# Low parts, loads and stores of two MLP products: which engine or queue makes them

## The chip, the core and the metric

The kernel runs on one core of a Trainium2 chip. A core has five engines, each with an instruction stream that runs in order: TensorE (PE in the profile; its weight loads are PEld), VectorE (DVE), ScalarE (ACT), GpSimd (POOL) and SyncE (SP). Transfers are issued from a stream too: plain loads from SP, and from POOL the stores and the accumulating loads, which add what they bring to what the tile holds. Sixteen DMA engines carry them. The metric is device time in microseconds.

## The reference

Two residual sub-layers over 1024 tokens of width 1024: a mixer (an RG-LRU and an S5 state space group), and then an MLP with a squared ReLU. Only the MLP is touched:

```python
x = layer_norm(DEEPNORM_ALPHA * x + g1 * m_lat, ln1_g[l], ln1_b[l])
f_lat = sq_relu_mlp(modulate(x, sh2, sc2), mlp_w1[l], mlp_b1[l], mlp_w2[l], mlp_b2[l])
x = layer_norm(DEEPNORM_ALPHA * x + g2 * f_lat, ln2_g[l], ln2_b[l])

def sq_relu_mlp(x, w1, b1, w2, b2):
    return jnp.square(jax.nn.relu(x @ w1 + b1)) @ w2 + b2
```

`w1` is 1024 x 4096, `w2` is 4096 x 1024, all in fp32.

## The kernel before

**Three products for one.** An fp32 operand is split into a high part `wh`, which ScalarE casts to the matmul type fp32r, and a low part `wl`, the remainder. A product is then high x high, high x low and low x high: three matmuls of 128x128 by 128x512.

**Seven products for eight.** Both MLP matrices are cut into 2 x 2 blocks and multiplied by a scheme of seven block products, named "1" to "7". Their operands are blocks or sums of blocks, and the results are added up in several steps.

**First product.** `w1` comes as 32 tiles of [128, 1024], two to a pair, 16 pairs. Product "2" of all pairs is made early, while the mixer ends, and its result goes to a DRAM scratch, `p2scr`. The other six follow in a loop over `stream`: for each pair p the products "1", "6", "7", "4", "5", "3", each of 12 matmuls into one PSUM bank (`part_product`, L1061 to L1067). `combo_next` (L1126) prepares operands four products ahead. `operand` builds the sums of w1 blocks on VectorE (`st`, `wr`). For "6", "7", "5" and "3" the low part is a VectorE subtraction. "1" and "4" are plain blocks of w1, and theirs comes another way:

```python
if n in "14":
    S.activation(lo, f(hi), AF.Copy, scale=-1.0)
    G.dma_start(out=lo, in_=a["w1"][2 * p + (n == "4")][:, HS[n == "4"]], accum_op=ADD)
```

that is, ScalarE writes minus the high part (L1137), and an accumulating load from POOL's queue adds the block of w1 to it, 256 KB (L1138). The tiles `wh` and `wl` hold two operands each and have three buffers, so six operands, one pair.

**What follows a product.** VectorE adds the PSUM bank to the running sums `u` and `r`; ScalarE applies ReLU and square into `hq`, four hidden blocks of a pair; after "3" VectorE adds four sums of hidden blocks (the operands of the second product) to the same tile, and POOL stores block 0 (L1187, 256 KB) and blocks 2 to 7 (L1188, 1.5 MB). Beside this, for 14 of the 16 pairs, two tiles of `w2` are loaded (`we` 512 KB, `wo` 256 KB, one buffer each), VectorE makes a sum of three of its blocks, and POOL stores that in `sscr` (L1195).

**Second product.** Seven products of seven units each (the 14 pairs). A unit loads a [128, 1024] tile of w2 into `wr` (three buffers), for "7", "5" and "3" a second one into `by`, which VectorE adds or subtracts; it splits the sum into `wh` and `wl`, loads the hidden block `br`, splits that into `bh` and `bl`, and runs 24 matmuls (L1267). `unit_next` prepares a unit ahead. `finish` (L1248) takes a finished quarter of the result through the residual: it loads a tile `nin`, scales and shifts it on VectorE (a tensor_scalar) and adds it to `acc`. The last two pairs, without the scheme, are added at the end (`weights2`, `hidden`, L1347).

**Order.** A scheduler places each engine's instructions by data and buffers, and the engines then run them in that order; an instruction that waits holds up all behind it on its engine or queue.

Of the kernel before, what the change touches and what calls it, by code (L numbers as in the profile page):

```python
# [7 lines left out]
F32 = mybir.dt.float32  # L8
# [33 lines left out]
def build(nc, tc, a, out):  # L42
# [15 lines left out]
    def ld(o, i):  # L58
        return nc.sync.dma_start(out=o, in_=i)
# [7 lines left out]
    def f(t):  # L67
        return t.bitcast(F32)
# [1003 lines left out]
    for p in range(0, NP1 + 4, 2):  # L1072
# [7 lines left out]
        for e in range(2):  # L1080
# [3 lines left out]
            t = ap_.tile([P, 512], F32, tag="r", name="p2", bufs=6)  # L1084
# [19 lines left out]
    raws, sums = {}, {}  # L1104

    def raw_of(i):
        if i not in raws:
            raws[i] = wp.tile([P, 1024], F32, tag="wr", name="wr", bufs=3)
            ld(raws[i], a["w1"][i])
        return raws[i]  # L1110

    def operand(n, p):
        if n == "1":
            x, y = raw_of(2 * p), raw_of(2 * p + 1)
# [11 lines left out]
    def combo_next():  # L1126
        while len(c_ahead) < 4 and c_n[0] < len(stream):
# [8 lines left out]
            if n in "14":  # L1136
                S.activation(lo, f(hi), AF.Copy, scale=-1.0)  # L1137
                G.dma_start(out=lo, in_=a["w1"][2 * p + (n == "4")][:, HS[n == "4"]], accum_op=ADD)  # L1138
            else:
                tt(lo, src_, f(hi), SUB)  # L1140
# [4 lines left out]
    us_, t1, hq = {}, {}, {}  # L1145

    def rt():
        return ap_.tile([P, 512], F32, tag="r", name="r", bufs=6)
# [5 lines left out]
    for n, p in stream:  # L1154
        w = combo_next()
        ps = bank(512, "ps_m1")
        part_product(ps, w, XS[n], True, True)
        if n == "1":

            hq[p] = a2.tile([P, 8, 512], F32, tag="hq", name="hq", bufs=2)  # L1160
            u = us_[p] = a1.tile([P, 2, 512], F32, tag="u", name="u", bufs=2)
            v, t = rt(), rt()
            ld(v, p2scr[p])
            S.copy(t, ps)
            tt(v, t, v, ADD)
            act(0, v, hq[p][:, 0])
        elif n == "6":
            tt(u[:, 1], ps, t, ADD)
        elif n == "7":
            tt(u[:, 0], ps, u[:, 1], ADD)  # L1170
        elif n == "4":
            v = rt()
            tt(v, ps, u[:, 0], ADD)
            act(1, v, hq[p][:, 3])
        elif n == "5":
            tt(u, ps.unsqueeze(1).to_broadcast([P, 2, 512]), u, ADD)
            act(1, u[:, 0], hq[p][:, 2])
        elif n == "3":
            tt(u[:, 1], ps, u[:, 1], ADD)
            act(0, u[:, 1], hq[p][:, 1])  # L1180
            h = hq[p]
            if p < NPAIR:
                tt(h[:, 4:6], h[:, 1:3], h[:, 0:2], SUB)
                tt(h[:, 6], h[:, 2], h[:, 4], SUB)
                tt(h[:, 7], h[:, 3], h[:, 6], SUB)
                hv = hscr[p // 2].rearrange("i p k c -> p i k c")[:, :, p % 2]
                G.dma_start(out=hv[:, 0], in_=h[:, 0])  # L1187
                G.dma_start(out=hv[:, 2:8], in_=h[:, 2:8])  # L1188
# [264 lines left out]
```

## Time and profile before

| | us |
|---|---|
| median of 3 runs (1666.52 to 1676.39) | 1667.84 |
| the profiled execution's own time | 1675.67 |
| its span, first to last instruction | 1673.9 |
| stretch of the first MLP product | 967 to 1324 |
| second MLP product | 1324 to 1615 |
| rest | 1615 to 1674 |

| engine | busy us | share of the span |
|---|---|---|
| PE | 1504.9 | 90% |
| DVE | 1258.8 | 75% |
| ACT | 850.6 | 51% |
| POOL | 74.7 | 4% |

A row of the profile's groups names a line of the kernel, an engine, an operation, output and inputs by the names of their tiles, and a count; behind it stand the busy time, the mean of one, and the idle time ahead of it with what ended that. PEclk is the granted clock of TensorE as a share of full speed. A busy TensorE may thus still run at less than its full clock. Line numbers of helpers (L47, a VectorE operation on two tensors; L59, a load on SP) hold many different operations, so names of tiles tell them apart.

### The profile page before, as it was taken

The page shows a single profiled execution, that of the slowest core. Times are in us where ns is not written, and L with a number is a line of the kernel's source. Part 1 is how long each engine was busy: PE and PEld are TensorE (multiplying, and loading weights), DVE is VectorE, ACT ScalarE, POOL GpSimd, SP SyncE. Part 2 cuts the span into 40 slices and gives each one's busy share as a digit, 9 for nine tenths or more (in the row PEclk, how much of TensorE's full clock was granted, in tenths as well). Part 3 has the DMA queues.
Part 4 walks back from the last instruction along what each step waited for, and adds up shares of the span by engine and source line. Part 5 has one row for each costly group of instructions (what it writes and reads, how often), then busy time and mean ns, then how long its engine had stood idle before and what let it go on. Part 6 is the DMA issues. An engine that isn't in the chain of part 4 may idle for free.

```text
span 1673.9 us, 20450 instructions
## 1 busy us (share of the span) xinstructions
PE 1504.9 (90%) x7148; PEld 1222.3 (73%) x7148; DVE 1258.8 (75%) x2546; ACT 850.6 (51%) x1194; POOL 74.7 (4%) x129
## 2 busy tenths in 40 slices
PE   7899998999879997899997997877888899999897
PEld 2687777777758786888786775666766688787687
DVE  7899999998949897449787885656565446658967
ACT  4666666666882327643335754435454433333315
POOL 0000000000000000000000121111111000000000
PEclk9999999999999999899999998888898999999898
DMA  7533333333745838837685777786665776867712
GB/s 255 209 117 110 104 107 116 116 122 120 266 161 160 224 114 201 200 141 237 210 269 163 240 211 228 246 252 194 176 176 168 248 249 211 282 206 249 267 44 101
DMA packets 138470, 312.55 MB, mean 187 GB/s; under 512 B 16384, under 2 KB 47616, under 8 KB 136960
## 3 DMA queue, kind: packets, MB, share of 16 engines
q1 hardware_dynamic: 109152, 245.31, 46.1%
q0 software_dynamic: 15168, 48.24, 9.9%
q10 hardware_dynamic: 14048, 17.70, 3.0%
q8 instruction: 56, 0.92, 0.2%
q14 instruction: 46, 0.38, 0.1%
HBM read 231.58 MB, written 79.63 MB: 186 GB/s over the span
## 4 chain that ended last, share of the span: by engine, by line
PE 34%; DVE 27%; DMA 17%; issue 11%; ACT 10%; POOL 1%; SPq 0%; ACTq 0%; DVEq 0%; POOLq 0%
PE ps_m L1267 13%; PE ps_mm L380 4%; PE ps_m L1066 4%; DMA wr<-in_w 4%; PE ps_g L435 3%; DMA mo<-in_ada_t 3%; DVE wl L47 3%; DVE sT L47 2%; DMA wl<-in_w 2%; DVE xc L56 2%; DVE ii L47 2%; PE ps_m L1347 2%; ACT H L603 2%; DVE sU L47 1%; DVE H L47 1%
## 5 line engine op out<-in xcount | busy, mean ns | idle before, releaser
L98 ACT CAST wh<-wr 128x1024 fp32r<-128x1024 f32 x113 | 118.6, 1052 | 256.5 <-PE ps_m L1267 84.5
L47 DVE TENSOR_TENSOR wl<-wr,wh 128x1024 fp32r<-128x1024 f32 (+1 forms) x129 | 148.7, 1154 | 90.9 <-ACT wh L98 80.4
L1066 PE MATMUL ps_m<-xt,wh 128*128 128x512 f32 x512 | 160.6, 396 | 0.0
L1267 PE MATMUL ps_m<-bh,wh 128*128 128x512 f32 x392 | 155.0, 397 | 5.4 <-ACT bh L1229 3.1
L1267 PE MATMUL ps_m<-bh,wl 128*128 128x512 f32 x392 | 153.0, 394 | 2.7 <-DVE wl L47 2.7
L1267 PE MATMUL ps_m<-bl,wh 128*128 128x512 f32 x392 | 154.1, 393 | 0.0
L380 PE MATMUL ps_mm<-x0h,wl 128*128 128x512 f32 x352 | 141.2, 402 | 0.9 <-DVE wl L47 0.9
L380 PE MATMUL ps_mm<-x0h,wh 128*128 128x512 f32 x352 | 141.0, 400 | 1.0 <-ACT wh L98 1.0
L380 PE MATMUL ps_mm<-x0l,wh 128*128 128x512 f32 x352 | 140.5, 399 | 0.0
L1066 PE MATMUL ps_m<-x,wl 128*128 128x512 f32 x128 | 62.4, 488 | 59.0 <-DMA wl<-in_w 59.0
L1066 PEld LDWEIGHTS ps_m<-xt,wh 128*128 128x128 f32 x512 | 99.2, 194 | 21.9 <-ACT wh L1135 0.2
L1066 PE MATMUL ps_m<-xt,wl 128*128 128x512 f32 x256 | 100.2, 393 | 1.0 <-DMA wl<-in_w 1.0
L1066 PE MATMUL ps_m<-x,wh 128*128 128x512 f32 x256 | 94.7, 456 | 0.0
L1267 PEld LDWEIGHTS ps_m<-bh,wh 128*128 128x128 f32 x392 | 74.8, 191 | 22.9 <-ACT bh L1229 3.6
L1267 PEld LDWEIGHTS ps_m<-bh,wl 128*128 128x128 f32 x392 | 74.3, 190 | 18.4 <-DVE wl L47 3.1
L1267 PEld LDWEIGHTS ps_m<-bl,wh 128*128 128x128 f32 x392 | 74.7, 191 | 15.9 <-issue 0.2
L675 PE MATMUL ps_wo<-ms,wh 128*128 128x512 f32 x256 | 81.1, 397 | 1.8 <-ACT ms L799 0.9
L1066 PEld LDWEIGHTS ps_m<-x,wl 128*128 128x128 f32 x128 | 29.7, 232 | 72.5 <-DMA wl<-in_w 65.6
L380 PEld LDWEIGHTS ps_mm<-x0h,wl 128*128 128x128 f32 x352 | 67.4, 192 | 14.3 <-DVE wl L47 1.4
L380 PEld LDWEIGHTS ps_mm<-x0h,wh 128*128 128x128 f32 x352 | 67.6, 192 | 13.7 <-ACT wh L98 1.4
L380 PEld LDWEIGHTS ps_mm<-x0l,wh 128*128 128x128 f32 x352 | 67.6, 192 | 12.9
L47 DVE TENSOR_TENSOR sT<-al,H 128x128 f32<-128x128 f32 x254 | 66.5, 284 | 1.3
(347 smaller groups left out, 3775.2 us busy)
## 6 DMA issues: line engine op xcount, KB each, us to landing
wr<-in_w SPq DMA_DIRECT2D x86, 512.0 KB, 4.4
br<-hq SPq DMA_DIRECT2D x49, 512.0 KB, 4.9
hq<-hq POOLq DMA_DIRECT2D x14, 1536.0 KB, 8.7
mo<-in_ada_t SPq DMA_DIRECT2D x32, 512.0 KB, 3.9
wr<-in_w_in SPq DMA_DIRECT2D x24, 512.0 KB, 4.5
wr<-in_w_out SPq DMA_DIRECT2D x24, 512.0 KB, 4.5
xt<-xt ACTq DMA_DIRECT2D x16, 512.0 KB, 2.7
yd<-Y SPq DMA_DIRECT2D x16, 512.0 KB, 2.6
```

The source lines that it names most:

```text
L47: (eng or V).tensor_tensor(out=o, in0=x, in1=y, op=op)
L56: V.scalar_tensor_tensor(out=o, in0=x, scalar=s, in1=y, op0=op0, op1=op1, **kw)
L98: S.copy(hi, raw)
L380: PE.matmul(ps, w[:, ks], x, start=(k == 0 and c == 0), stop=(k == KT - 1 and c == 2))
L435: PE.matmul(ps, w[:, w0:w0 + P], x[:, src:src + n], start=(c == 0), stop=(c == 2))
L603: S.copy(hv[0:64], ps[0:64])
L675: PE.matmul(ps, u[:, ks], v[:, js], start=(c == 0), stop=(c == 3 * KT - 1))
L1066: PE.matmul(ps, u[:, ks], v, start=(first and c == 0), stop=(last and c == 11))
L1267: PE.matmul(pss[m], w[:, 512 * k + P * m:512 * k + P * m + P], x[:, 512 * k:512 * k + 512], start=(q == 0 and k == 0 and c == 0), stop=(q ...
L1347: PE.matmul(ps, w[:, m * P:(m + 1) * P], x[:, js], start=(c == 0), stop=(c == 3 * len(hs) - 1))
```

## The change

In the first product:

- The low parts of "1" and "4" are made by VectorE like all others; the negation and the accumulating load are gone.
- `load_pair` loads a pair's two w1 tiles, its `p2` block and its two w2 tiles when "4" of the pair before is prepared. The w1 tiles have five buffers, three `wr` and two `wr2`; `p2t` has two; `we` and `wo` keep one.
- The first hidden block adds PSUM to `p2t` directly, where it took ScalarE's copy of it.
- The sum of w2 blocks is made after "7" into a tile of its own, `w2s` (one buffer), with its sign turned, and the products that use it follow.
- `hq` holds four blocks, and the four sums get a tile `hs` (one buffer). The stores are block 0 after "6" (256 KB), blocks 2 and 3 after "3" (512 KB), and `hs` (1 MB).

In the second product "5" and "3" get their sum from an accumulating load by POOL (14 of 512 KB) and no `by`; "7" keeps it. `finish` scales `nin` on ScalarE.

```diff
@@ -1081,7 +1081,7 @@
             es_ = slice(512 * e, 512 * e + 512)
             ps = bank(512, "ps_p2")
             part_product(ps, (wh[:, es_], wl[:, es_]), x0[1::2], True, True)
-            t = ap_.tile([P, 512], F32, tag="r", name="p2", bufs=6)
+            t = ap_.tile([P, 512], F32, tag="r", name="p2", bufs=4)
             S.copy(t, ps)
             G.dma_start(out=p2scr[p - 4 + e], in_=t)
     for _ in steps:
@@ -1101,17 +1101,31 @@
         return t.rearrange("p (k c) -> p k c", k=2)
 
     stream = [(n, p) for p in range(NP1) for n in "167453"]
-    raws, sums = {}, {}
-
-    def raw_of(i):
-        if i not in raws:
-            raws[i] = wp.tile([P, 1024], F32, tag="wr", name="wr", bufs=3)
+    raws, sums, p2t, w2t = {}, {}, {}, {}
+
+    def load_pair(p):
+        for i in (2 * p, 2 * p + 1):
+            pl_, tag, bf = (wp, "wr", 3) if i % 5 < 3 else (a1, "wr2", 2)
+            raws[i] = pl_.tile([P, 1024], F32, tag=tag, name="wr", bufs=bf)
             ld(raws[i], a["w1"][i])
-        return raws[i]
+
+        p2t[p] = a1.tile([P, 512], F32, tag="p2", name="p2t", bufs=2)
+        ld(p2t[p], p2scr[p])
+        if p < NPAIR:
+            e = a1.tile([P, 1024], F32, tag="we", name="we", bufs=1)
+            o = a1.tile([P, 512], F32, tag="wo", name="wo", bufs=1)
+            ld(two(e), a["w2"][2 * p:2 * p + 2, :, HI].rearrange("k p c -> p k c"))
+            ld(o, a["w2"][2 * p][:, LO])
+            w2t[p] = e, o
 
     def operand(n, p):
         if n == "1":
-            x, y = raw_of(2 * p), raw_of(2 * p + 1)
+            if p == 0:
+                load_pair(0)
+        if n == "4" and p + 1 < NP1:
+            load_pair(p + 1)
+        if n == "1":
+            x, y = raws[2 * p], raws[2 * p + 1]
             s2, s3, s4 = (a1.tile([P, 512], F32, tag="st", name=f"st{i}", bufs=4) for i in range(3))
             tt(s3, x[:, LO], y[:, LO], SUB)
             tt(y[:, LO], y[:, LO], y[:, HI], ADD)
@@ -1133,19 +1147,13 @@
             src_ = operand(n, p)
             hi, lo = (x[:, HS[c % 2]] for x in c_tile[0])
             S.copy(hi, src_)
-            if n in "14":
-                S.activation(lo, f(hi), AF.Copy, scale=-1.0)
-                G.dma_start(out=lo, in_=a["w1"][2 * p + (n == "4")][:, HS[n == "4"]], accum_op=ADD)
-            else:
-                tt(lo, src_, f(hi), SUB)
+            tt(lo, src_, f(hi), SUB)
             c_ahead.append((hi, lo))
         return c_ahead.pop(0)
 
     XS = {"1": x0[0::2], "5": xt_[0], "6": xt_[1], "7": xt_[2], "3": x1, "4": xt_[3]}
-    us_, t1, hq = {}, {}, {}
-
     def rt():
-        return ap_.tile([P, 512], F32, tag="r", name="r", bufs=6)
+        return ap_.tile([P, 512], F32, tag="r", name="r", bufs=4)
 
     def act(e, v, dst):
         S.activation(v, v, AF.Relu, bias=col("b1", 2 * p + e))
@@ -1155,46 +1163,46 @@
         w = combo_next()
         ps = bank(512, "ps_m1")
         part_product(ps, w, XS[n], True, True)
+        hv = hscr[p // 2].rearrange("i p k c -> p i k c")[:, :, p % 2] if p < NPAIR else None
         if n == "1":
 
-            hq[p] = a2.tile([P, 8, 512], F32, tag="hq", name="hq", bufs=2)
-            u = us_[p] = a1.tile([P, 2, 512], F32, tag="u", name="u", bufs=2)
-            v, t = rt(), rt()
-            ld(v, p2scr[p])
+            h = a2.tile([P, 4, 512], F32, tag="hq", name="hq", bufs=2)
+            u = a1.tile([P, 2, 512], F32, tag="u", name="u", bufs=2)
+            v, t = p2t.pop(p), rt()
             S.copy(t, ps)
-            tt(v, t, v, ADD)
-            act(0, v, hq[p][:, 0])
+            tt(v, ps, v, ADD)
+            act(0, v, h[:, 0])
         elif n == "6":
             tt(u[:, 1], ps, t, ADD)
+            if hv is not None:
+                G.dma_start(out=hv[:, 0], in_=h[:, 0])
         elif n == "7":
             tt(u[:, 0], ps, u[:, 1], ADD)
+            if hv is not None:
+                e, o = w2t.pop(p)
+                w2s = a1.tile([P, 512], F32, tag="ws", name="w2s", bufs=1)
+                tt(e[:, LO], e[:, LO], e[:, HI], ADD)
+                tt(w2s, o, e[:, LO], SUB)
+                G.dma_start(out=sscr[p // 2][:, p % 2], in_=w2s)
         elif n == "4":
             v = rt()
             tt(v, ps, u[:, 0], ADD)
-            act(1, v, hq[p][:, 3])
+            act(1, v, h[:, 3])
         elif n == "5":
             tt(u, ps.unsqueeze(1).to_broadcast([P, 2, 512]), u, ADD)
-            act(1, u[:, 0], hq[p][:, 2])
+            act(1, u[:, 0], h[:, 2])
         elif n == "3":
             tt(u[:, 1], ps, u[:, 1], ADD)
-            act(0, u[:, 1], hq[p][:, 1])
-            h = hq[p]
-            if p < NPAIR:
-                tt(h[:, 4:6], h[:, 1:3], h[:, 0:2], SUB)
-                tt(h[:, 6], h[:, 2], h[:, 4], SUB)
-                tt(h[:, 7], h[:, 3], h[:, 6], SUB)
-                hv = hscr[p // 2].rearrange("i p k c -> p i k c")[:, :, p % 2]
-                G.dma_start(out=hv[:, 0], in_=h[:, 0])
-                G.dma_start(out=hv[:, 2:8], in_=h[:, 2:8])
-                e = a1.tile([P, 1024], F32, tag="we", name="we", bufs=1)
-                o = a1.tile([P, 512], F32, tag="wo", name="wo", bufs=1)
-                ld(two(e), a["w2"][2 * p:2 * p + 2, :, HI].rearrange("k p c -> p k c"))
-                ld(o, a["w2"][2 * p][:, LO])
-                tt(e[:, LO], e[:, LO], e[:, HI], ADD)
-                tt(o, e[:, LO], o, SUB)
-                G.dma_start(out=sscr[p // 2][:, p % 2], in_=o)
+            act(0, u[:, 1], h[:, 1])
+            if hv is None:
+                G.dma_start(out=hx[p - NPAIR], in_=h)
             else:
-                G.dma_start(out=hx[p - NPAIR], in_=h[:, 0:4])
+                G.dma_start(out=hv[:, 2:4], in_=h[:, 2:4])
+                x = a2.tile([P, 4, 512], F32, tag="hs", name="hs", bufs=1)
+                tt(x[:, 0:2], h[:, 1:3], h[:, 0:2], SUB)
+                tt(x[:, 2], x[:, 0], h[:, 2], SUB)
+                tt(x[:, 3], h[:, 3], x[:, 2], ADD)
+                G.dma_start(out=hv[:, 4:8], in_=x)
     ast.close()
     x2st.close()
 
@@ -1207,7 +1215,7 @@
     W = {(i, k): [a["w2"][4 * q + k:4 * q + 4:2, :, HS[i]].rearrange("k p c -> p k c") for q in range(NPAIR // 2)]
          for i in range(2) for k in range(2)}
     PRODUCTS = (("1", (W[0, 0],), 0), ("2", (W[0, 1],), 3), ("6", (sscr,), 6), ("7", (W[0, 0], W[1, 0], SUB), 5), ("4", (W[1, 1],), 7),
-                ("5", (W[1, 0], W[1, 1], ADD), 4), ("3", (W[0, 1], sscr, SUB), 2))
+                ("5", (W[1, 0], W[1, 1]), 4), ("3", (W[0, 1], sscr), 2))
     NQ = NPAIR // 2
     units = [(u, v, q) for n, u, v in PRODUCTS for q in range(NQ)]
     u_n, u_ahead = [0], []
@@ -1218,7 +1226,9 @@
             u_n[0] += 1
             raw = wp.tile([P, 1024], F32, tag="wr", name="wr2", bufs=3)
             ld(two(raw), u[0][q])
-            if len(u) > 1:
+            if len(u) == 2:
+                G.dma_start(out=two(raw), in_=u[1][q], accum_op=ADD)
+            elif len(u) > 2:
                 by = bp.tile([P, 1024], F32, tag="by", name="by", bufs=2)
                 ld(two(by), u[1][q])
                 tt(raw, raw, by, u[2])
@@ -1250,7 +1260,7 @@
         ac = acc_of(m, j)
         nt = mp.tile([P, 512], F32, tag="r", name="nin", bufs=3)
         ld(nt, nscr[m, j])
-        ts(nt, nt, cr[:, m:m + 1], MUL, cd[:, m:m + 1], ADD)
+        S.activation(nt, nt, AF.Identity, bias=cd[:, m:m + 1], scale=cr[:, m:m + 1])
         stt(ac, ac, g2c[:, m:m + 1], nt, MUL, ADD)
         if j not in centres:
             centres[j] = centre(512)
```

On POOL's queue, in the middle of the first product of the kernel before (`hq_9063` and its like are the scratch of a pair of pairs in DRAM):

```order
L1188 DMA hq_9063<-hq 128x6x512
L1138 DMA wl<-in_w 128x512
L1187 DMA hq_9064<-hq 128x512
L1138 DMA wl<-in_w 128x512
L1188 DMA hq_9064<-hq 128x6x512
```

In the changed kernel at about the same place:

```order
L1205 DMA hq_9065<-hs 128x4x512
L1200 DMA hq_9065<-hq 128x2x512
L1178 DMA hq_9066<-hq 128x512
L1205 DMA hq_9065<-hs 128x4x512
L1200 DMA hq_9066<-hq 128x2x512
```

The accumulating loads of `wl`, which stood between the stores, are gone, and the 1.5 MB store has become one of 1 MB (L1205) and one of 512 KB (L1200).

On VectorE, a middle pair of the kernel before, from behind the sum that follows "6" (`st` with the lowest number of its three is the operand of "6", the next of "7", the last of "3"; `u<-ps_m` and `r<-ps_m` are the sums that follow a product):

```order
L47 TENSOR_TENSOR we<-we 128x512
L47 TENSOR_TENSOR wl<-st_10015,wh 128x512
L47 TENSOR_TENSOR wo<-we,wo 128x512
L47 TENSOR_TENSOR u<-ps_m_9995,u 128x512
L47 TENSOR_TENSOR st_10158<-wr 128x512
L47 TENSOR_TENSOR wr<-wr 128x512
L47 TENSOR_TENSOR r<-ps_m_10025,u 128x512
L47 TENSOR_TENSOR wl<-st_10016,wh 128x512
L47 TENSOR_TENSOR st_10157<-wr 128x512
L47 TENSOR_TENSOR we<-we 128x512
L47 TENSOR_TENSOR st_10159<-wr,st_10157 128x512
L47 TENSOR_TENSOR u<-ps_m_10044,u 128x1024
```

The same place in the changed kernel:

```order
L47 TENSOR_TENSOR wl<-wr,wh 128x512
L47 TENSOR_TENSOR wl<-st_10034,wh 128x512
L47 TENSOR_TENSOR we<-we 128x512
L47 TENSOR_TENSOR u<-ps_m_10014,u 128x512
L47 TENSOR_TENSOR st_10177<-wr 128x512
L47 TENSOR_TENSOR w2s<-wo,we 128x512
L47 TENSOR_TENSOR r<-ps_m_10043,u 128x512
L47 TENSOR_TENSOR wl<-st_10035,wh 128x512
L47 TENSOR_TENSOR wl<-wr,wh 128x512
L47 TENSOR_TENSOR st_10179<-wr,st_10177 128x512
L47 TENSOR_TENSOR u<-ps_m_10062,u 128x1024
L47 TENSOR_TENSOR we<-we 128x512
```

The low part of "1" of the next pair (the first row) has come in ahead of that of "6", that of "4" stands behind that of "7", and between two `we` rows there are now five rows behind the `w2s` sum.

On POOL's queue, where the first product ends and the second begins, in the changed kernel:

```order
L1198 DMA hx_9074<-hq 128x2048
L1198 DMA hx_9075<-hq 128x2048
L1230 DMA wr_12683<-in_w 128x2x512
L1230 DMA wr_12777<-in_w 128x2x512
L1230 DMA wr_12814<-in_w 128x2x512
```

Behind the last two stores of the first product stand only the accumulating loads of the second.

## Rows read from the trace of the kernel before

**Rows 1.** Busy us (xrows) of PE, PEld, DVE, ACT, POOL; PEclk, DMA share, GB/s.

```profile
967.00:1150.00 183.00, 146.15 (x580) 115.68 (x578) 115.94 (x174) 76.92 (x134) 33.67 (x47) 0.90 0.76 235
...
1324.00:1515.00 191.00, 189.56 (x828) 156.52 (x829) 112.17 (x109) 73.39 (x75) 0.00 (x0) 0.99 0.75 249
1515.00:1615.00 100.00, 90.17 (x379) 72.66 (x378) 82.92 (x105) 32.29 (x32) 0.00 (x0) 0.93 0.63 208
```

**Rows 2.** Timeline of PE, second product, 150 rows apart: start, us, name.

```profile
1365.94 0.39 PE L1267 MATMUL ps_m<-bh,wh 128*128 128x512 f32 x1
...
1399.94 0.39 PE L1267 MATMUL ps_m<-bh,wh 128*128 128x512 f32 x1
```

**Rows 3.** Timeline of PE: first row of the first product, and of the second.

```profile
967.17 0.63 PE L1066 MATMUL ps_m<-x,wh 128*128 128x512 f32 x2
...
1324.11 1.22 PE L1267 MATMUL ps_m<-bh,wh 128*128 128x512 f32 x2 [3.13 <-ACT bh L1229]
```

**Rows 4.** Waits of PE, 967 to 1324: us in total, times, longest.

```profile
PE ps_m L1066 <- DMA wl<-in_w: 60.0, 16, 11.5
```

**Rows 5.** Timeline 1138 to 1152, POOL and PE rows.

```profile
1138.87 0.84 POOL L1188 DMA_DIRECT2D hq<-hq  x1 [3.00 <-DVE u L47]
...
1147.75 0.90 POOL L1138 DMA_DIRECT2D wl<-in_w  x1 [8.03 <-issue]
...
1151.59 0.79 PE L1066 MATMUL ps_m<-x,wl 128*128 128x512 f32 x1 [7.91 <-DMA wl<-in_w]
```

**Rows 6.** Waits of POOL and DVE, 967 to 1324.

```profile
POOL wl L1138 <- issue: 87.3, 12, 9.3
...
DVE we L47 <- DMA we<-in_w: 23.4, 10, 5.0
```

**Rows 7.** DMA issues 967 to 1321: count, KB each, median us to landing.

```profile
hq<-hq POOLq DMA_DIRECT2D x14, 1536.0 KB, 8.7
wr<-in_w SPq DMA_DIRECT2D x34, 512.0 KB, 4.4
wl<-in_w POOLq DMA_DIRECT2D x32, 256.0 KB, 4.2
...
ws<-wo POOLq DMA_DIRECT2D x14, 256.0 KB, 4.7
```

**Rows 8.** Timeline of DVE at the start of the first product.

```profile
968.55 2.49 DVE L47 TENSOR_TENSOR x<-b,x 128x512 fp32r<-128x512 f32 x4
```

**Rows 9.** Timeline of DVE, three rows on end: start, us.

```profile
1060.16 0.68 DVE L47 TENSOR_TENSOR wo<-we,wo 128x512 f32<-128x512 f32 x1
1060.76 1.22 DVE L47 TENSOR_TENSOR hq<-hq 128x1024 f32<-128x1024 f32 x1
1061.89 0.68 DVE L47 TENSOR_TENSOR r<-r 128x512 f32<-128x512 f32 x1
```

**Rows 10.** Tile `we`: landing of its loads.

```profile
DMA to landing us min/median/max: 3.8/5.3/8.5
```

**Rows 11.** Busy us of a stretch with two w2 sums a pair (columns of rows 1).

```profile
1034.00:1104.00 70.00, 60.20 (x226) 47.71 (x226) 40.03 (x60) 27.24 (x47) 12.94 (x18) 0.87 0.80 249
```

**Rows 12.** Lines of PE, 1324 to 1615: busy us, mean ns | idle before.

```profile
L1267 PE MATMUL ps_m<-bh,wh 128*128 128x512 f32 x392 | 155.0, 397 | 5.4 <-ACT bh L1229 3.1 <-DVE u L47 1.3 <-DVE acc L47 0.9
...
L1267 PE MATMUL ps_m<-bh,wl 128*128 128x512 f32 x392 | 153.0, 394 | 2.7 <-DVE wl L47 2.7
L1347 PE MATMUL ps_m<-hh,w2h 128*128 128x256 f32 x7 | 2.4, 358 | 2.8 <-ACT w2h L1308 2.8
L1347 PE MATMUL ps_m<-hh,w2l 128*128 128x256 f32 x7 | 2.4, 420 | 2.9 <-DVE w2l L56 1.9 <-DVE wm L51 1.1
```

**Rows 13.** Lines of DVE, 1515 to 1615: busy us, mean ns.

```profile
L47 DVE TENSOR_TENSOR wr<-wr,by 128x1024 f32<-128x1024 f32 x13 | 15.7, 1217 | 0.2
...
L53 DVE TENSOR_SCALAR nin<-nin,c 128x512 f32<-128x512 f32 x8 | 4.2, 538 | 1.0 <-DMA nin<-n 1.0
```

**Rows 14.** Tile `mh` (512 KB accumulating loads, in the mixer): landing.

```profile
DMA to landing us min/median/max: 6.3/7.9/10.7
```


## What the change does to the time

> **What bounds it now.** I read the busy shares by stretch first [rows 1]. The kernel ends on TensorE, and the two MLP products fill the last 707 us. In the second product (from 1324) TensorE is busy nearly throughout at the upper clock level, 0.99 granted. In the first (967 to 1324) it is not: 146 of 183 us, clock 0.90. That is the stretch with slack, and only its waits can be shortened by much.
>
> How large is the slack? At a granted clock of 1.00 matmuls start every 0.2267 us: 150 steps between the two rows [rows 2]. The first product has 16 pairs x 6 products x 12 = 1152 matmuls, so it needs 1152 x 0.2267 = 261.1 us. It takes 356.9, from its first matmul at 967.17 to the first of the second product at 1324.11 [rows 3]. Of the 95.8 us lost, the waits name 60.0 us in 16 waits, every one for a DMA into `wl` [rows 4], and 3.1 at the change of stage [rows 3]. The other 32.7 have no waiter: they are matmuls at the lower of the clock's two levels (1.2 against 2.4 GHz) after each wait: in [rows 5] a wait of 7.91 ends at 1151.59, and the matmul behind it takes 0.79 us, against 0.39 in [rows 2]. So each us of wait costs 95.8 / 63.1 = 1.52 us.
>
> Why is `wl` late? [rows 5] shows one such case. POOL issues the 1.5 MB store at 1138.87, and its next instruction, the accumulating load of the low part of "1", goes out only at 1147.75 after 8.03 us of "issue"; four us later TensorE moves. It is no accident: POOL stood so before L1138 12 times, 87.3 us in all [rows 6]. The 1.5 MB store takes 8.7 us to land and the 256 KB accumulate 4.2 more [rows 7]. The wait is a queue behind a big store, not weight traffic as such.
>
> **The change part by part.**
>
> *Low parts on VectorE.* 32 POOL DMAs and 32 ScalarE negations go; 32 VectorE rows come. Low part and store no longer share a queue, so the 60.0 us of waits and their share of the slow clock go as a whole: the stage would be 261.1 plus what comes new. The w1 tiles that come a pair earlier and the fewer `r` tiles (now two a pair) I price at nothing: no wait of TensorE names either [rows 4].
>
> *New, pair 0.* VectorE now makes this low part after the x parts, which end at 968.55 + 2.49 = 971.0 [rows 8]. TensorE asks for it four matmuls after 967.17, at 968.1, and gets it one row later at 971.6: 3.5 us. The low part of "6" stands ninth after the x parts, 971.0 + 9 x 0.60 = 976.4; TensorE reaches it at 974.0, having 8 matmuls of "1" and two of "6" ahead: 2.4 us. Together 5.9 x 1.52 = 9.0 us. Later pairs have cover: the low parts of "1" and "6" of the next pair stand right after "6" of this one, so "7", "4", "5" and "3" of this pair (48 x 0.2267 = 10.9 us) lie ahead of their use; less three rows, 9 us of slack.
>
> *VectorE's own load.* A row of 512 columns starts 0.60 us after the one before, a row of 1024 takes 1.13 [rows 9]. A pair now has 21 short and 2 long rows where it carries two w2 sums (six pairs, 2 to 7): 14.9 us. TensorE needs 72 x 0.2267 = 16.3 us per pair. So VectorE fits, by 1.4 us, as long as it waits for nothing. The last eight pairs carry no w2 sums (4 rows less, 12.5 us) and need no price. The direct read of PSUM for the first hidden block takes ScalarE's copy out of VectorE's way; I take nothing for it.
>
> *w2 loads.* `we` and `wo` have one buffer each, so the second load of a pair is issued after the first `w2s` sum and VectorE meets its `we` row 4 short rows and a long one later: 3.5 us. The next pair's first load has 11 short and one long row of cover, 7.7 us. With a landing time L, the pair lasts 14.9 + (L - 3.5) + (L - 7.7, if positive). Before, `we` landed in 3.8 to 8.5 us, 5.3 in the median [rows 10], and VectorE already stood 23.4 us waiting for it [rows 6]. L = 5.3 gives 16.7, L = 8.5 gives 20.7. Since the loads now meet a shorter pair I take the middle, 6.9: 18.3 us, 2.0 above TensorE. Six pairs give 12.0, less the 9 of slack, 3.0 x 1.52 = 4.6 us. `w2s` too has one buffer; its store lands in 4.7 [rows 7], less than L, and is hidden behind it.
>
> *DMA bandwidth.* A pair with two w2 sums moves 1.0 MiB of w1, 0.25 of p2, 1.5 of w2, 1.75 of h stores and 0.5 of ws, 5.24 MB. The fullest stretch of before moved 249 GB/s at a DMA share of 0.80 [rows 11], thus some 311 at a full share: 16.8 us per pair, already inside the 18.3. The Trainium skill, "DMA: Bandwidth & Descriptors", Specifications, gives a limit of about 358 GB/s per core; by it (an estimate) a pair would need 14.6 us, the loads could keep their 5.3, and the first product would come to 274.8, the time to 1582. No run here shows 358; the row's ceiling stands behind the sum.
>
> *Smaller stores.* The same bytes in three pieces (256 KB, 512 KB, 1 MB). Nothing that TensorE waits for stands behind them any more, except `hs` (one buffer, written once a pair, 16 us apart against 8.7 for 1.5 MB): nothing. If that cover failed, VectorE would stop at `hs`, which is the case of L = 8.5 below.
>
> The first product: 261.1 + 9.0 + 4.6 + 4.7 (the 3.1 at its end, x 1.52) = 279.4, against 356.9: -77.5 us.
>
> *Second product.* 14 VectorE sums of 128x1024 go (1217 ns each in [rows 13]; 14 x 1.13 = 15.8 us of starts) and some of the 538 ns scalings of `nin` move to ScalarE, which is busy 32 of 100 us there [rows 1]. VectorE is busy 83 of these 100. TensorE's waits in the whole product, without the first 3.1, add to 10.7 [rows 12]; all gone, x 1.52 = -16.6. Against it: a buffer is now held for a load of 4.4 [rows 7], then an accumulating load of 512 KB, whose nearest row is 6.3 to 10.7 [rows 14], then a cast and a low part (a long row of 1.13 each, [rows 9]) and up to three long rows of others ahead in VectorE's order: 13.0 to 20.8 us over three buffers, 4.3 to 6.9 per unit, where TensorE needs 24 x 0.2267 = 5.44. At the long end 14 x 1.46 = 20.4, less the two units in the other buffers (10.9), x 1.52 = +14. I take half of the waits of L1347 (2.8 + 2.9), 5.7 / 2 x 1.52 = -4: these come right after VectorE's full stretch, and the other end needs every accumulate late.
>
> Sum: -77.5 - 4 = -81.5 on the profiled execution's own 1675.7 (its span of 1673.9 and 1.8 around it), that is 1594.2. That execution is 7.8 above the median of 1667.8; carried over, 1586.
>
> **The rivals.**
>
> R1, w2 loads set the pair. For it: VectorE's waits for `we` before [rows 6]. Against: the median landing. At L = 8.5 six pairs of 20.7 are 26.4 over, less 9, x 1.52 = 26.4; stage 301.2, gain 55.7 + 4, thus 1608.
>
> R2, the accumulating DMAs starve the second product: +14 in place of -4. For it: 10.7 in [rows 14]. Against: with the median of 7.9 a unit takes 4.9 to 6.0, and 14 x 0.6 = 8 lies inside the two units. Then 1675.7 - 77.5 + 14 - 7.8 = 1604.
>
> R3, the stall only changes its cause. Low parts stand in VectorE's order behind w2 sums as they stood behind the store on POOL. At L = 11 a pair lasts 25.7, six are 56.4 over, less 9, x 1.52 = 72, stage 346.8: 1654, within 1%. For it: the order itself. Against: no `we` above 8.5.
>
> R4, slower. The same queue on VectorE, past its break-even: the stage equals 356.9 when the six pairs lose (356.9 - 274.8) / 1.52 + 9 = 63 us, 10.5 each, at L = 11.6. At L = 13 the stage is 383 and the time 1690. For it: two loads in series per pair behind 5.24 MB of traffic. Against: it needs one and a half times the longest landing seen.
>
> **How the numbers follow.** My forecast holds 0.65, R1 0.13, R2 0.14, R3 0.05, R4 0.03. The forecast's own range is 1569 (L = 5.3: 274.8, -82.1 - 16.6) to 1594 (L = 7.7: 286.7). With R1 and R2, and both at once (-55.7 + 14, thus 1626), the range is 1569 to 1626. A measurement of this kernel tells about 1%, 17 us, from no change: faster is the forecast with R1 and R2, 0.92; same R3, 0.05; slower R4, 0.03.
>
> **What would show it.** Right: no wait of TensorE for a DMA into `wl`; waits for VectorE's `wl` at pair 0 and small ones in pairs 2 to 7; the first product near 280 us at a granted clock above 0.97; the pairs after 8 near 16.3. Wrong: `we` landing above 8 us with VectorE waiting for it (R1, R3, R4); in the second product TensorE waiting for `wh` whose cast waits for a DMA into `wr` (R2); a granted clock that stays at 0.9 though the waits are gone, which would leave up to 32.7 us unrecovered.

## The result, and the profile after

The changed kernel takes 1611.15 us (median of 4 runs, 1604.65 to 1614.26) against 1671.2 (4 runs, 1666.52 to 1676.39), a ratio of 0.9635, 95% interval 0.9589 to 0.968: 3.65% faster. The forecast was 1586, its range 1569 to 1626. The profiled execution has a span of 1609.2 us, 64.7 less than the 1673.9 of before.

Where did the 64.7 us come from? The two MLP products moved in opposite directions. First the busy shares by stretch of the changed kernel (columns as in [rows 1]: us, PE, PEld, DVE, ACT and POOL busy with their counts, PEclk, DMA share, GB/s):

```profile
966.00:1110.00 144.00, 137.02 (x583) 109.48 (x582) 122.69 (x189) 69.99 (x117) 23.04 (x37) 0.99 0.79 269
1110.00:1244.00 134.00, 130.87 (x572) 106.73 (x571) 103.34 (x149) 77.71 (x127) 14.90 (x22) 1.00 0.58 197
1244.00:1435.00 191.00, 191.00 (x835) 157.94 (x836) 108.59 (x102) 80.64 (x83) 1.22 (x1) 0.99 0.75 244
1435.00:1535.00 100.00, 76.07 (x296) 57.88 (x296) 58.83 (x76) 32.20 (x34) 13.26 (x13) 0.90 0.81 210
```

The first product (966 to 1244) now runs at a granted clock of 0.99 and 1.00, and TensorE is idle in it for 10 us only. The second product starts as before, at 0.99 without a gap until 1435. But in the next 100 us TensorE is busy 76 us at a clock of 0.90, where [rows 1] had 90 us at 0.93.

The limits of the first product, in the timeline of TensorE (first row of the first product, end of its longest wait, first row of the second product):

```profile
965.86 0.63 PE L1066 MATMUL ps_m<-x,wh 128*128 128x512 f32 x2
...
970.39 0.50 PE L1066 MATMUL ps_m<-x,wl 128*128 128x512 f32 x1 [3.44 <-DVE wl L47]
...
1243.97 2.07 PE L1277 MATMUL ps_m<-bh,wh 128*128 128x512 f32 x4 [3.13 <-ACT bh L1239]
```

1243.97 - 965.86 = 278.1 us, against 356.9 in [rows 3]: 78.8 us gained. The rest, from there to the end of the span, is 1609.2 - 1243.97 = 365.2 against 1673.9 - 1324.11 = 349.8: 15.4 us lost. (The remaining 1.3 us lie ahead of the first product.)

What TensorE waits for in the first product:

```profile
PE ps_m L1066 <- DVE wl L47: 7.0, 6, 3.4
PE ps_m L1277 <- ACT bh L1239: 3.1, 1, 3.1
```

The 60.0 us for a DMA into `wl` of [rows 4] are gone. In their place stand 7.0 us for VectorE's `wl`, and the 3.1 at the change of stage are as they were. In the second product the longest waits are new:

```profile
PE ps_m L1277 <- ACT wh L98: 8.7, 3, 5.5
PE ps_m L1277 <- DVE wl L47: 7.1, 4, 5.6
PE ps_m L1277 <- DVE u L47: 5.5, 1, 5.5
```

And its DMA issues (count, KB each, median us to landing), plain loads from SP and accumulating loads from POOL:

```profile
wr<-in_w SPq DMA_DIRECT2D x41, 512.0 KB, 4.6
...
wr<-in_w POOLq DMA_DIRECT2D x7, 512.0 KB, 6.3
wr<-ws POOLq DMA_DIRECT2D x7, 512.0 KB, 6.5
```

The accumulating loads land in 6.3 and 6.5 us in the median (5.3 to 10.7 over all 14); the bounds taken from [rows 14] were 6.3 to 10.7.

### The profile page after: what moved, and what is told of

It is laid out like the page before. It is cut to its first block, busy times and chain, and to the rows that moved or that the text cites. A ratio compares the mean times of both kernels' runs of the same rounds, so it can differ in the third digit from the quotient of the medians.

```text
span 1609.2 us, 20405 instructions
## 1 busy us (share of the span) xinstructions
PE 1480.6 (92%) x7148; PEld 1203.4 (75%) x7148; DVE 1249.8 (78%) x2548; ACT 844.4 (52%) x1178; POOL 69.2 (4%) x125
## 4 chain that ended last, share of the span: by engine, by line
PE 50%; DVE 21%; DMA 15%; ACT 7%; issue 6%; SPq 0%; ACTq 0%; DVEq 0%; POOLq 0%; POOL 0%
PE ps_m L1277 12%; PE ps_m L1066 10%; PE ps_mm L380 7%; PE ps_g L435 4%; PE ps_wo L675 3%; DMA wr<-in_w 3%; DMA mo<-in_ada_t 3%; DVE wl L47 2%; DMA we<-in_w 2%; PE ps_wo L694 2%; PE ps_m L1357 2%; PE ps_p L1066 2%; DVE xc L56 2%; DVE ii L47 2%; ACT H L603 2%
## 5 line engine op out<-in xcount | busy, mean ns | idle before, releaser
L47 DVE TENSOR_TENSOR wl<-wr,wh 128x1024 fp32r<-128x1024 f32 (+1 forms) x161 | 171.1, 1064 | 117.2 <-ACT wh L98 112.9
L1066 PE MATMUL ps_m<-xt,wh 128*128 128x512 f32 x512 | 158.0, 390 | 0.0
L1066 PEld LDWEIGHTS ps_m<-xt,wh 128*128 128x128 f32 x512 | 96.2, 188 | 20.6 <-ACT wh L1149 0.2
L1066 PE MATMUL ps_m<-xt,wl 128*128 128x512 f32 x256 | 99.9, 391 | 2.8 <-DVE wl L47 2.8
L1066 PE MATMUL ps_m<-x,wh 128*128 128x512 f32 x256 | 81.4, 399 | 0.0
L601 PE MATMUL ps_si<-ub,xt 128*128 128x160 f32 x256 | 47.5, 328 | 14.4 <-ACT H L606 11.6
L675 PE MATMUL ps_gl<-G,wh 128*128 128x512 f32 x192 | 60.5, 396 | 0.1
```

The source lines that it names most:

```text
L47: (eng or V).tensor_tensor(out=o, in0=x, in1=y, op=op)
L601: last_in[m] = PE.matmul(ps[:, i, :], xt[:, g, i, :], ub[:, 4 * q + g, :], start=True, stop=True)
L675: PE.matmul(ps, u[:, ks], v[:, js], start=(c == 0), stop=(c == 3 * KT - 1))
L1066: PE.matmul(ps, u[:, ks], v, start=(first and c == 0), stop=(last and c == 11))
```

## Experiments

All lengths of the first product below run from the first matmul of L1066 on `ps_m` to the first of the second product, in the profiled execution; "the rest" is from there to the end of the span. Ratios are to the kernel before, run beside it.

### The second product

Four kernels tell apart the sums by DMA, the scaling of `nin`, and an effect of the first product on the second.

**e1_first_only**: both edits of the second product undone.

```diff
-                ("5", (W[1, 0], W[1, 1]), 4), ("3", (W[0, 1], sscr), 2))
+                ("5", (W[1, 0], W[1, 1], ADD), 4), ("3", (W[0, 1], sscr, ADD), 2))
...
-        S.activation(nt, nt, AF.Identity, bias=cd[:, m:m + 1], scale=cr[:, m:m + 1])
+        ts(nt, nt, cr[:, m:m + 1], MUL, cd[:, m:m + 1], ADD)
```

> The changed kernel with its second product as in the kernel before: the sums of "5" and "3" by a load into `by` and a VectorE addition, and `nin` scaled on VectorE. Theory A (the accumulating loads cost the second product what it lost): from its first matmul to the end 350 us as before, not 365, so about 1595 us. Theory B (a faster first product hands the second its own delay, through traffic or late stores): it stays at 1608 to 1612.

**e2_sums_by**: only the first of these two edits. 

> The changed kernel with only the sums of "5" and "3" taken back to `by` and VectorE; `nin` stays on ScalarE. Theory A: about 1595 us, the waits of TensorE for `wh` and `wl` (8.7 and 7.1 us) and the 5.5 put down to `u` gone. Theory B: 1608 to 1612. Theory C (`nin` on ScalarE holds up the casts behind it in its queue): 1603 to 1611.

**e3_nin_dve**: only the second. 

> The changed kernel with only `nin` taken back to VectorE; sums by accumulating loads. Theory A: no change, 1608 to 1613. Theory C: 1597 to 1603, with TensorE's waits for `wh` gone.

**e4_second_only**: the kernel before with the second product of the changed one (its hidden sum and w2 sum with the turned sign).

```diff
-            if len(u) > 1:
+            if len(u) == 2:
+                G.dma_start(out=two(raw), in_=u[1][q], accum_op=ADD)
+            elif len(u) > 2:
...
-        ts(nt, nt, cr[:, m:m + 1], MUL, cd[:, m:m + 1], ADD)
+        S.activation(nt, nt, AF.Identity, bias=cd[:, m:m + 1], scale=cr[:, m:m + 1])
```

> The kernel before with only the second product changed (accumulating loads in "5" and "3", `nin` on ScalarE). Theory A: 13 to 18 us above before, about 1684. Theory B: like before, 1665 to 1675, since its first product is the slow one.

| kernel | us | ratio (interval) | first product | the rest |
|---|---|---|---|---|
| before | | | 356.9 | 349.8 |
| after | 1611.15 | 0.9635 (0.9589 to 0.968) | 278.1 | 365.2 |
| e1_first_only | 1595.91 | 0.9524 (0.950 to 0.9548) | 277.7 | 346.3 |
| e2_sums_by | 1596.8 | 0.9505 (0.9479 to 0.953) | 278.9 | 343.2 |
| e3_nin_dve | 1613.38 | 0.9617 (0.9595 to 0.964) | 279.6 | 363.5 |
| e4_second_only | 1691.22 | 1.0082 (1.0058 to 1.0106) | 358.5 | 363.6 |

Theory A holds in all four (e3_nin_dve lies 0.4 us above its range; e4_second_only is 14.3 us above the 1676.95 of the kernel before beside it). Wherever the accumulating loads are, the rest takes 363.5 to 365.2 us, whatever the first product does; without them 343.2 to 346.3. The waits agree. TensorE's waits in the second product of e2_sums_by:

```profile
PE ps_m L1277 <- DVE wl L47: 0.8, 1, 0.8
...
PE ps_m L1277 <- ACT wh L98: 0.4, 1, 0.4
```

In e3_nin_dve:

```profile
PE ps_m L1277 <- ACT wh L98: 11.4, 3, 5.7
PE ps_m L1277 <- DVE u L47: 6.1, 1, 6.1
```

In e4_second_only:

```profile
PE ps_m L1269 <- DVE u L47: 6.8, 1, 6.8
PE ps_m L1269 <- ACT wh L98: 6.6, 4, 4.0
```

TensorE waits for the cast of the weights (6.6 and 11.4 us) and for the `u` of the product before (6.1 and 6.8 us) in the two kernels with accumulating loads; in e2_sums_by the first wait is 0.4 us and the second is gone. Theories B and C fall. Scaling `nin` on ScalarE costs nothing and gains, if anything, 3 us of the rest (343.2 against 346.3), less than the measured times tell apart.

**Why do they cost?** In the changed kernel, the casts of the accumulated weights on ScalarE (start, us, and the idle time ahead with what ended it):

```profile
1446.21 1.04 ACT L98 CAST wh<-wr 128x1024 fp32r<-128x1024 f32 x1 [11.42 <-DMA wr<-in_w]
...
1452.27 1.05 ACT L98 CAST wh<-wr 128x1024 fp32r<-128x1024 f32 x1 [4.07 <-DMA wr<-in_w]
...
1458.65 1.05 ACT L98 CAST wh<-wr 128x1024 fp32r<-128x1024 f32 x1 [4.61 <-DMA wr<-in_w]
...
1464.77 1.05 ACT L98 CAST wh<-wr 128x1024 fp32r<-128x1024 f32 x1 [2.46 <-DMA wr<-in_w]
...
1474.61 1.04 ACT L98 CAST wh<-wr 128x1024 fp32r<-128x1024 f32 x1 [4.35 <-DMA wr<-in_w]
```

and the accumulating loads on POOL:

```profile
1446.46 1.18 POOL L1230 DMA_DIRECT2D wr<-in_w  x1 [9.81 <-DMA nin<-n]
1452.53 1.20 POOL L1230 DMA_DIRECT2D wr<-in_w  x1 [4.89 <-issue]
1458.87 1.19 POOL L1230 DMA_DIRECT2D wr<-in_w  x1 [5.14 <-issue]
1465.01 1.20 POOL L1230 DMA_DIRECT2D wr<-in_w  x1 [4.95 <-issue]
1474.86 1.19 POOL L1230 DMA_DIRECT2D wr<-in_w  x1 [8.65 <-issue]
```

These are the last five of the seven loads of "5". Each goes out 0.2 to 0.3 us after the cast that shows that the one before has landed: they run one at a time. They follow at 6.1 to 9.9 us, and TensorE needs a unit every 5.44. It is not that their tiles come late. SP's plain loads go out as soon as the low part of three units earlier has freed a tile:

```profile
1456.03 5.34 SPq L59 DMA_DIRECT2D wr<-in_w  x2
```

By that order the second of these two, out by 1461.37, fills the tile to which the load of 1474.86 adds, 13.5 us later. Why POOL waits for the one before, the trace names only as "issue" (and for the first of the five as `nin`, which lands at that time too).

It is not a rule for accumulating loads as such. In the kernel before, two of 256 KB leave POOL 1.13 us apart, though the first takes 3.9 us to land:

```profile
1170.05 0.87 POOL L1138 DMA_DIRECT2D wl<-in_w  x1 [8.54 <-issue]
...
1171.18 1.21 POOL L1138 DMA_DIRECT2D wl<-in_w  x1
```

And in e6_low_only (below), which has no accumulating load in its first product, a plain store waits in the same way, up to 8.4 us:

```profile
POOL ws L1191 <- issue: 15.6, 2, 8.4
```

The loads of "3" do overlap: one leaves at 1503.83 and takes 5.8 us to land, the next leaves at 1506.37. One difference from those of "5" is the number of packets for the same 512 KB. POOL's queue moved 272 packets in the time of one load of "5", and 288 in the time of two loads of "3" (packets, MB, share of the 16 engines):

```profile
q0 software_dynamic: 272, 0.52, 54.9%
...
q0 software_dynamic: 288, 1.05, 46.8%
```

So a limit on how many pieces POOL may have under way would fit these rows. No run varies that number, and it is not shown.

**e5_five_bufs**: every other accumulated unit in a `by` tile.

```diff
-            raw = wp.tile([P, 1024], F32, tag="wr", name="wr2", bufs=3)
+            if len(u) == 2 and q % 2:
+                raw = bp.tile([P, 1024], F32, tag="by", name="by", bufs=2)
+            else:
+                raw = wp.tile([P, 1024], F32, tag="wr", name="wr2", bufs=3)
```

> The changed kernel, with every other accumulated unit of "5" and "3" put into a `by` tile (2 buffers, unused there), so five buffers in place of three; sums still by accumulating loads. Theory A1 (a unit's chain of load, accumulating load, cast and low part, some 18 us, over three buffers is longer than TensorE's 5.44 us a unit): five buffers give 3.6 us a unit, the waits go, about 1594 to 1599 us. Theory A2 (the accumulates are late by traffic or by the order of ScalarE's and VectorE's queues, not by buffers): it stays at 1606 to 1613.

1598.9 us, 0.9529 (0.9502 to 0.9556); first product 278.6, the rest 348.7. TensorE's waits in the second product:

```profile
PE ps_m L1280 <- DVE u L47: 7.3, 1, 7.3
```

The landing of its 14 accumulating loads:

```profile
DMA to landing us min/median/max: 5.5/8.4/10.5
```

The time is that of theory A1, and the waits for `wh` are gone, although the loads land later than in the changed kernel (8.4 us in the median, 6.4 there). But A1's working, 3.6 us a unit, is not what ran. On POOL:

```profile
1379.54 1.22 POOL L1233 DMA_DIRECT2D by<-in_w  x1 [130.95 <-DMA wr<-in_w]
1390.42 1.21 POOL L1233 DMA_DIRECT2D by<-in_w  x1 [9.66 <-DVE bl L47]
1420.41 1.18 POOL L1233 DMA_DIRECT2D wr<-in_w  x1 [28.78 <-DMA wr<-in_w]
...
1450.67 1.19 POOL L1233 DMA_DIRECT2D wr<-in_w  x1 [9.66 <-DMA nin<-n]
1456.57 1.20 POOL L1233 DMA_DIRECT2D by<-in_w  x1 [4.70 <-DVE cs L47]
1467.22 1.19 POOL L1233 DMA_DIRECT2D wr<-in_w  x1 [9.46 <-issue]
```

The first two loads of "5" go out 41 and 30 us ahead of the third, into `by` tiles that stood empty. The later ones still follow one another at 5.9 and 10.7 us, the last after 9.46 us of "issue". So what the two tiles bought is a head start of two units of seven, which TensorE then eats up. One wait of 7.3 us remains, put down to `u`.

### The first product

The diff's edits there are four: the low parts, the loads of w1 a pair ahead, the smaller stores (with `p2t`), and the order of the w2 loads.

**e6_low_only**: the kernel before with the low parts of "1" and "4" on VectorE, nothing else.

```diff
-            if n in "14":
-                S.activation(lo, f(hi), AF.Copy, scale=-1.0)
-                G.dma_start(out=lo, in_=a["w1"][2 * p + (n == "4")][:, HS[n == "4"]], accum_op=ADD)
-            else:
-                tt(lo, src_, f(hi), SUB)
+            tt(lo, src_, f(hi), SUB)
```

> The kernel before with only the low parts of "1" and "4" made by VectorE; the 1.5 MB store, the loads and `r` tiles as before. Theory D1 (the queue behind the store was the whole loss): the first product falls from 357 to 278 to 290 us, about 1600 to 1610 in all. Theory D2 (the earlier loads and the smaller stores carry a good part): 300 to 325 us, 1620 to 1645.

**e7_low_dma**: the changed kernel with that one edit undone. 

> The changed kernel with only the low parts of "1" and "4" back on ScalarE and the accumulating load. On POOL they stand behind the 1 MB store (8.1 us to landing) in place of the 1.5 MB one. Theory D1: TensorE again waits for a DMA into `wl` once a pair, 40 to 60 us in all, the first product 335 to 360, 1665 to 1690. Theory D2: 285 to 310, 1618 to 1645.

**e9_late_loads**: e2_sums_by with the w1 loads of before.

```diff
-        for i in (2 * p, 2 * p + 1):
-            pl_, tag, bf = (wp, "wr", 3) if i % 5 < 3 else (a1, "wr2", 2)
-            raws[i] = pl_.tile([P, 1024], F32, tag=tag, name="wr", bufs=bf)
-            ld(raws[i], a["w1"][i])
...
+            for i in (2 * p, 2 * p + 1):
+                raws[i] = wp.tile([P, 1024], F32, tag="wr", name="wr", bufs=3)
+                ld(raws[i], a["w1"][i])
```

> The kernel of e2_sums_by with the two w1 tiles of a pair loaded as in the kernel before (three buffers, when "1" is prepared); low parts on VectorE and small stores stay. e6_low_only, without both, took 302 us for the first product against 279. Theory F1 (there VectorE's waits for w1 tiles, 42 us, held the low parts behind them): the first product takes 295 to 305 us here too, about 1612 to 1624 in all. Theory F2 (the 1.5 MB store was what was late there, in traffic or in buffers): 277 to 285 us, 1595 to 1604.

**e10_stores_only**: e9 with the low parts as before, too. 

> e9 with the low parts of "1" and "4" back on the accumulating load: of the first product's changes the smaller stores stay (with `p2t`, the w2 loads and `r`), while low parts and w1 loads are as before. e7_low_dma, with the early loads too, took 307 us against 357 before. Theory G1 (the smaller store ahead of the accumulating load made that gain): 305 to 320 us, 1625 to 1640 in all. Theory G2 (the early w1 loads made it): 340 to 357 us, 1655 to 1672.

| kernel | low parts "1", "4" | w1 loads | stores | first product | us | ratio (interval) |
|---|---|---|---|---|---|---|
| before | by DMA | as before | large | 356.9 | | |
| e6_low_only | VectorE | as before | large | 302.5 | 1627.35 | 0.9689 (0.9659 to 0.972) |
| e10_stores_only | by DMA | as before | small | 303.9 | 1618.75 | 0.9645 (0.9625 to 0.9665) |
| e9_late_loads | VectorE | as before | small | 302.6 | 1614.15 | 0.9619 (0.9592 to 0.9645) |
| e7_low_dma | by DMA | a pair ahead | small | 307.5 | 1641.45 | 0.9772 (0.9741 to 0.9804) |
| after | VectorE | a pair ahead | small | 278.1 | 1611.15 | 0.9635 (0.9589 to 0.968) |

(The second product is that of before in e6, that of e2_sums_by in e9 and e10, and that of the changed kernel in e7; the first products are what is compared.) e6, e9 and e10 lie at 302 to 304: either the low parts or the smaller stores (with `p2t` and the w2 loads, which e10 does not tell apart from them) take away the queue behind the large store, 53 to 54 us, and the second of them then adds nothing. What stands next is another wait. In e6_low_only (waits of all engines in the first product):

```profile
DVE st L47 <- DMA wr<-in_w: 42.4, 12, 5.4
...
PE ps_m L1066 <- DVE wl L47: 20.5, 10, 4.5
```

VectorE waits 42.4 us for w1 tiles, and the low parts are behind it in order. In e9_late_loads one such case, on VectorE:

```profile
1101.34 0.69 DVE L47 TENSOR_TENSOR st<-wr 128x512 f32<-128x512 f32 x1 [2.34 <-DMA wr<-in_w]
...
1102.55 0.68 DVE L47 TENSOR_TENSOR wl<-st,wh 128x512 fp32r<-128x512 f32 x1
```

The `st` at 1101.34 waits 2.34 us for its w1 tile, and behind it, at 1102.55, comes the low part for which TensorE then waits until 1103.29. With the w1 tiles a pair ahead that wait is not there, and the first product falls by another 24 us. e6_low_only and e7_low_dma both lie in the ranges of D2, and D1 falls: the queue behind the store was 54 us of the 79, not the whole. F1 holds (302.6), and F2 falls. G1 is the nearer for e10_stores_only, which lies below its ranges (303.9 where it had 305 to 320, 1618.75 where it had 1625 to 1640) and far from those of G2. It keeps the accumulating load for the low parts, and

```profile
PE ps_m L1066 <- DMA wl<-in_w: 23.1, 12, 4.1
...
POOL wl L1150 <- issue: 14.9, 14, 5.5
```

POOL's "issue" ahead of it is 14.9 us where [rows 6] had 87.3, with 5.5 us as the longest where it had 9.3. The early w1 loads add nothing to such a kernel: e7_low_dma has them too, and 307.5. Early loads without the smaller stores were not tried.

**e8_no_w2**, **e11_we_twice** and **e12_paced** are made on e2_sums_by and ask what is left, the w2 loads.

e8_no_w2 loads `we` and `wo` for the first pair only, and so leaves out the w2 sums of 13 pairs:

```diff
+            if p == 0:
...
+                w2t[-1] = e, o
+            w2t[p] = w2t[-1]
```

> The kernel of e2_sums_by without the loads of `we` and `wo` after the first pair (the sums are made from the same tiles, so 13 pairs' w2 sums are left out in value and the output is another). The prediction priced the wait for these loads at 4.6 us, with 9 us of cover: then VectorE's 18.8 us of waits for `we` and TensorE's two gaps of 1.8 us near 1082 and 1101 go, and the time falls by 3 to 7 us to 1590 to 1594. If the loads cost more by traffic, 1580 to 1588; if the waits are all covered, 1595 to 1598.

1587.99 us, 0.9453 (0.9418 to 0.9488); first product 272.8. In the changed kernel VectorE waited for these loads:

```profile
DVE we L47 <- DMA we<-in_w: 18.8, 6, 4.3
```

In e8_no_w2 TensorE's wait for VectorE's low parts in the first product is only that of the first pair, 3.4 of 3.6 us:

```profile
PE ps_m L1066 <- DVE wl L47: 3.6, 2, 3.4
```

272.8 against 278.9 in e2_sums_by: 6.1 us, where the prediction had 4.6. The whole time lies 2 us under the range for the waits and at the end of that for traffic; this run takes away waits and traffic together and does not tell them apart.

e11_we_twice issues each load of `we` twice (`for _ in range(2):` ahead of its `ld`). 

> The kernel of e2_sums_by with each load of `we` issued twice, one after the other, so that its landing time L about doubles, from 5.4 to some 10.5 us. The prediction's rule, 14.9 + (L - 3.5) + (L - 7.7) us a pair in six pairs, gives 24.7 us a pair, 50 us over TensorE's 16.3, less 9 of slack, x 1.52 = 63: the first product at about 340 us and 1655 to 1660 in all. If TensorE's waits cover the loads better than that rule has it: 290 to 315 us, 1608 to 1635.

1620.4 us, 0.9661 (0.9636 to 0.9686); first product 304.6, not 340. The waits:

```profile
DVE we L47 <- DMA we<-in_w: 51.4, 12, 6.1
...
PE ps_m L1066 <- ACT wh L1150: 14.5, 7, 3.0
```

VectorE's wait for `we` rises from 19.5 us in 6 times (e2_sums_by) to 51.4 in 12. But the scheduler placed the w2 sums of the later pairs one to a pair, with a `we` row nine rows behind the `w2s` sum. So the rule for two sums in six pairs was not what ran, and this run does not test it; it shows that late w2 loads do reach TensorE.

e12_paced puts `w2s` into the ring of `p2t`, which makes the order one w2 sum a pair:

```diff
-        p2t[p] = a1.tile([P, 512], F32, tag="p2", name="p2t", bufs=2)
+        p2t[p] = a1.tile([P, 512], F32, tag="p2", name="p2t", bufs=3)
...
-                w2s = a1.tile([P, 512], F32, tag="ws", name="w2s", bufs=1)
+                w2s = a1.tile([P, 512], F32, tag="p2", name="w2s", bufs=3)
```

> The kernel of e2_sums_by with `w2s` in the ring of `p2t` (three buffers there in place of two and one), so that the order has one w2 sum a pair for 14 pairs in place of two in six pairs. Theory H1 (what is left of the wait for w2 loads comes from two loads in series inside one pair): VectorE's waits for `we` and TensorE's gaps after pair 0 go, and the first product falls from 279 to 271 to 274 us, as without the loads in e8_no_w2 (273); 0.945 to 0.949 of before. Theory H2 (the loads' traffic costs, not their order): 277 to 280 us, 0.950 to 0.953.

Neither range came: 1612.35 us, 0.9615 (0.9585 to 0.9645), first product 298.1 (971.12 to 1269.23). On VectorE, a middle pair (the sum, the row ahead of `we`, and `we`):

```profile
1058.52 0.68 DVE L47 TENSOR_TENSOR w2s<-wo,we 128x512 f32<-128x512 f32 x1
...
1062.12 0.69 DVE L47 TENSOR_TENSOR st<-wr,st 128x512 f32<-128x512 f32 x1
1066.80 0.69 DVE L47 TENSOR_TENSOR we<-we 128x512 f32<-128x512 f32 x1 [4.00 <-DMA we<-in_w]
```

Between the `w2s` sum that frees the tile and the next `we` row stand six rows of 0.60 us, 3.6 in all (the last is the second one shown), and the load needs longer. From the fifth pair on it is so in every pair, and VectorE waits 44.5 us in 11 times. All loads of `we`:

```profile
DMA to landing us min/median/max: 4.7/7.7/8.7
```

Both H1 and H2 fall. One sum a pair does not help when the order puts only 3.6 us of work between the sum that frees the tile and the row that needs the next load. But the landing counts as well: in the changed kernel the six loads that VectorE waits for land in 6.4 to 7.8 us, the other eight in 4.3 to 5.2. Why the one kind lands later, no run shows.

## Why the prediction was right, and where it was not

**What bounds the kernel.** Right. The waits for `wl` made the slow clock too: the first product lost 95.8 us on 63.1 of waits, and the factor of 1.52 held roughly. After, it loses 278.1 - 261.1 = 17.0 us on 10.1 of waits (1.7); e6_low_only 41.4 on 26.3 (1.6), e10_stores_only 42.8 on 26.2 (1.6). Of the 32.7 us that no wait named, 6.9 are left, at granted clocks of 0.99 and 1.00.

**The first product.** 279.4 forecast, 278.1 measured; -77.5 forecast, -78.8 measured. Pair 0: 5.9 us of wait forecast; 3.44 came for "1" (3.5 forecast), and in the changed kernel none of the 2.4 for "6". Six pairs with w2 sums: 4.6 forecast, 6.1 by e8_no_w2, which is an upper end, since its traffic is gone too. The landing time of `we`, taken as 6.9, is 5.1 in the median of all 14 loads, but 6.4 to 7.8 in the six that VectorE waited for, so this step held; none came near 8.5, and R1 and the two rivals beyond it did not come.

**The step that failed in the first product, without harm to the sum,** is "the w1 tiles that come a pair earlier ... I price at nothing: no wait of TensorE names either". VectorE's waits for w1 (22.0 us in 11 times before) lay beneath the larger stall, so TensorE's waits did not name them. With that stall gone and the loads where they were, they come to TensorE and cost 24 us (e9_late_loads against e2_sums_by). The low parts alone, to which the prediction gave the whole 60 us of waits, gain 54 us of 79. And they are not needed for that: the smaller stores, priced at nothing as well, gain 53 with the low parts as before (e10_stores_only, with `p2t` and the w2 loads of the changed kernel).

**The second product.** -4 forecast, +15.4 measured. This is where the point forecast missed, and why 1611 lies outside the forecast's own range of 1569 to 1594; the stated range holds it only by R1 and R2. 1586 with +15 in place of -4 would be 1605. The other 6 us are mostly the 7.8 that were taken off to get from the profiled execution to the median: the changed kernel's profiled execution lies at its median (1611.02), and beside the experiments the kernel before had medians of 1676.6 to 1679.3, so the 1667.8 of three runs was low.

The failed step is the choice between its two ends, "the other end needs every accumulate late". The sign that the prediction named for R2 came: the cast of `wh` waits for a DMA into `wr`. But that R2's +14 is so near is luck, since it was worked out from another cause, loads that land in 10.7 us. In the median they landed in 6.3 and 6.5 us, the short end of [rows 14]. The error was to spread a unit's chain over three buffers as if the accumulating loads could overlap: in "5", five of the seven went out only when the one before had landed, 6.1 to 9.9 us apart, as the rows of POOL show. The trace of before had a sign of it in the 8.03 us of "issue" in [rows 5]. The prediction read that, rightly, as a queue behind the large store, and did not ask whether the loads that it put on POOL would queue behind one another.

The relief of VectorE, for which the -4 stood, is not seen: with the sums on VectorE and only `nin` moved, the rest is 343.2 against 346.3 in e1_first_only, less than the measured times tell apart. (In the working of the range's lower end, 10.7 x 1.52 is 16.3, not 16.6; that moves it by 0.3 us.)

**Bandwidth.** The first product's first part moved 269 GB/s at a share of 0.79, thus 340 at a full share; the ceiling of 311 from [rows 11] was too low. The limit of about 358 GB/s of the Trainium skill ("DMA: Bandwidth & Descriptors", Specifications) is nearer, and below the 372 of a row in the last section; the measurement decides.

**The best version** of these runs is the changed kernel with its sums left to VectorE in the second product: e2_sums_by, 0.9505, and e1_first_only, 0.9524, not told apart; both beat the changed kernel's 0.9635. e5_five_bufs, which keeps the accumulating loads and gives them two more tiles, is not told apart from them either (0.9529).

## What to carry to other kernels

When the longest wait of the bounding engine is removed, the waits of the engines that feed it, hidden until then, are what is late next: price every wait of a feeder in that stretch as if it were uncovered, and the edit that removes it along with it. An accumulating load in place of a sum trades 1.1 us of an engine for a second landing in series; where such loads run one at a time, that landing (6 us here) is a rate, and it has to be under the time of a unit (5.4 us), or they need a head start. A tile with one buffer is paid for in the distance, in the order of the engine that frees it, between the row that frees it and the row that needs it again.

## What the runs showed of the hardware

Accumulating loads of 512 KB landed in 6.3 and 6.5 us in the median beside plain ones in 4.6, and in e5_five_bufs in 8.4.

Some of POOL's transfers left only 0.3 us after an earlier one had landed. Five loads of "5" in the changed kernel did (rows above). So did the load in [rows 5]: the store out at 1138.87 took 8.6 us to land, and the load followed at 1147.75. Others overlapped. The first load of "3", from the scratch of w2 sums, went out 0.70 us after the last of "5" (1475.56), and POOL's waits named "issue" before these 14 loads were 23.6 us in 4 times, all in "5". The plain store of e6_low_only shows that it is not a matter of accumulating alone. The numbers of packets let one suspect a limit on the pieces under way; the runs leave it open.

At the change of stage one core moved 372 GB/s for 20 us, with its DMA engines busy throughout (columns as above):

```profile
1240.00:1260.00 20.00, 16.86 (x67) 13.51 (x66) 11.27 (x10) 10.93 (x13) 0.55 (x1) 0.91 1.00 372
```
